# mLSTM gate sums taken once per block for each kind, and rows of z by transposes, in a one-core hybrid decoder trunk

## The chip, the cores and the metric

The kernel runs on one core of a Trainium2 chip. The metric is the device time of one execution in microseconds (us). The engines are named as in the profile: PE is TensorE (matrix products; PEld its weight loads), DVE is VectorE, ACT is ScalarE, POOL is GpSimd, SP is SyncE, whose queue issues most DMAs.

## The reference

One layer of a decoder trunk: an input norm, one input projection of a 1024-token sequence (width 1024, 16 learned meta tokens ahead of it), four mixers side by side (causal pooling, RWKV-7, RG-LRU, mLSTM; 4 heads of 64 each), one output projection, and a squared-ReLU MLP of width 4096, with two norms, all in float32. The part at issue is the mLSTM's gates:

```python
logi = jnp.where(valid, gates[..., :N_H], NEG)
logf = jnp.where(valid, jax.nn.log_sigmoid(gates[..., N_H:]), 0.0)
b = jnp.cumsum(logf, axis=2)                 # prefix sums over the tokens of a chunk
dmat = jnp.where(causal, b[:, :, :, None, :] - b[:, :, None, :, :] + logi[:, :, None, :, :], NEG)
m_intra = jnp.max(dmat, axis=3)              # needs the running maximum of z = logi - b
b_last = b[:, :, -1]                         # the sum over the whole chunk
```

## The kernel before

The 1024 tokens are worked on in 4 blocks of two chunks of 128 tokens; block 0 has the 16 meta tokens as a third, short chunk ahead. A string of steps (PLAN) sets the order in which the program emits its work. The steps of a block are the projection sweeps (S), the pooling (O), the RG-LRU (L), RWKV's preparation (P), its triangular inverse (I), its chunks (C) and outputs (c), mLSTM's gates (M b.0), chunks (M b.1 and on) and outputs (m), and the output projection (W). The first half of the MLP (G, 16 steps) and the first pieces of its second half (D) are put between the steps of the later blocks. After these steps, from about 800 us on, the second half of the MLP runs alone: products of whole tiles at L1189. The build interleaves the emitted steps on each engine; it takes the program as a whole, so an instruction more or less in one step can change how later steps stand against each other.

Large products are made of three: each float32 operand is split into a high and a low part of a reduced format (ACT casts to whi, L127 and L132; DVE subtracts to get wlo, L128 and L133), and high x high, low x high and high x low are summed in PSUM. L476 to L478 are the sweeps' products, L1167 to L1169 the output projection's, L1189 the MLP's. A float32 product outside of that scheme shows as two passes in the trace, a transpose as one; L188 is the transpose of the residual stream.

The change lies in mlstm_pre, the step M b.0. It computes for each chunk the log forget gate lf and the log input gate li, 4 columns (heads) a chunk, tokens on partitions. L952 multiplies by the lower-triangular matrix tri: prefix sums of lf. L953 multiplies by ones: the chunk's total on all partitions. Both write one PSUM tile pb, [128, 2, chunks, 4]; DVE copies it out (L955, L956) and subtracts (z = li - b, L958). L961 turns z into rows, a product with the identity that lands as [4, tokens], and DVE's scan at L964 takes the running maximum from those rows. L967 sums lf into columns. The PSUM tiles of these steps have the tag "l", which has one buffer, so that each of these tiles waits for the reading of the one before. For b = 0 the list `parts` holds the meta rows (16 partitions, chunk 0) and the rest (128 partitions, chunks 1 and 2); for other blocks one part with two chunks.

Two other places come up. The inverse (I) solves a triangular system on DVE (L781 and L782, alternating), stores the result to DRAM (L730, dr<-ys), reads it back in another layout (L733, SA<-dr, and L736, both on SP's queue), transposes it (DVE L739, ys<-SA) and hands it to PE (L748). L1033, L1046 and L1051 are products of mLSTM's chunk, L1040 and L1053 their readers on DVE, L908 to L914 the head norm of its output, whose L140 on POOL is the power -1/2. L1069 transposes that output for the output projection; L1172 adds the projection's result to the residual x. L1220 (POOL's queue) are loads of 1 MB that add a block of weights into DRAM sums (rd<-in_w); L1208 and L1209 add and store other sums (m, md).

Of the kernel before, what the change touches and what calls it, by code (L numbers as in the profile page):

```python
# [16 lines left out]
P = 128  # L17
# [80 lines left out]
class Trunk:  # L98
# [818 lines left out]
    def mlstm_pre(self, b):  # L917

        nc, ml, mp = self.nc, self.mls[b], self.mlp_
        mo, nb, ch = self.block(b)  # L920
        nch = len(ch)
        m = 1 if mo else 0
        li = ml["li"] = mp.tile([P, NTB + 1, NH], F32, name="ml_li", bufs=2)
        lf = ml["lf"] = mp.tile([P, NTB + 1, NH], F32, name="ml_lf", bufs=2)
        bt = ml["b"] = mp.tile([P, NTB + 1, NH], F32, name="ml_b", bufs=2)
        bl = ml["bl"] = mp.tile([P, NTB + 1, NH], F32, name="ml_bl", bufs=2)
        z = ml["z"] = mp.tile([P, NTB + 1, NH], F32, name="ml_z", bufs=2)
        cmr = ml["cm"] = mp.tile([16, NBM], F32, name="ml_g", bufs=2)[0:NH]
        blr = ml["blr"] = mp.tile([NH, NTB + 1], F32, name="ml_blr", bufs=2)
        xf = mp.tile([P, NTB + 1, NH], F32, name="ml_xf")  # L930
        ab = mp.tile([P, NTB + 1, NH], F32, name="ml_ab")
        pg = self.ps("l", [P, nch, 8])
        for ci, (c0, L, _, t) in enumerate(ch):
            nc.tensor.matmul(pg[0:L, ci], lhsT=ml["g"][:, c0:c0 + L], rhs=self.sel, start=True, stop=True)

        if mo:
            nc.vector.memset(li[:, 0], 0.0)
            nc.vector.memset(xf[:, 0], 0.0)
        parts = ([(slice(0, NM), 0, 1)] if mo else []) + [(slice(0, P), m, nch)]
        for rs, i0, i1 in parts:  # L940
            sh = [rs.stop, i1 - i0, NH]
            ifb = self.ifb[rs].rearrange("p (a b) -> p a b", a=1)
            nc.vector.tensor_tensor(li[rs, i0:i1], pg[rs, i0:i1, 0:4], ifb[:, :, 0:4].broadcast_to(sh), op=ALU.add)
            nc.vector.tensor_tensor(xf[rs, i0:i1], pg[rs, i0:i1, 4:8], ifb[:, :, 4:8].broadcast_to(sh), op=ALU.add)
        X = xf[:, 0:nch].rearrange("p a b -> p (a b)")
        AB = ab[:, 0:nch].rearrange("p a b -> p (a b)")
        nc.vector.scalar_tensor_tensor(AB, X, -1.0, X, op0=ALU.mult, op1=ALU.max)
        l1 = self.log1p_exp_neg(AB, [P, nch * NH], mp)
        nc.vector.scalar_tensor_tensor(lf[:, 0:nch].rearrange("p a b -> p (a b)"), X, 0.0, l1, op0=ALU.min, op1=ALU.subtract)
        pb = self.ps("l", [P, 2, nch, NH])  # L950
        for ci, (c0, L, _, t) in enumerate(ch):
            nc.tensor.matmul(pb[0:L, 0, ci], lhsT=self.tri[0:L, 0:L], rhs=lf[0:L, ci], start=True, stop=True)  # L952
            nc.tensor.matmul(pb[:, 1, ci], lhsT=self.ones[0:L].broadcast_to([L, P]), rhs=lf[0:L, ci], start=True, stop=True)  # L953
        for rs, i0, i1 in parts:
            nc.vector.tensor_copy(bt[rs, i0:i1], pb[rs, 0, i0:i1])  # L955
        nc.vector.tensor_copy(bl[:, 0:nch], pb[:, 1])  # L956
        for rs, i0, i1 in parts:
            nc.vector.tensor_tensor(z[rs, i0:i1], li[rs, i0:i1], bt[rs, i0:i1], op=ALU.subtract)  # L958
        pr = self.ps("l", [NH, nb])
        for ci, (c0, L, _, t) in enumerate(ch):  # L960
            nc.tensor.matmul(pr[:, c0:c0 + L], lhsT=z[0:L, ci], rhs=self.ident[0:L, 0:L], start=True, stop=True)  # L961
        for ci, (c0, L, _, t) in enumerate(ch):

            nc.vector.tensor_tensor_scan(cmr[:, c0:c0 + L], pr[:, c0:c0 + L], self.ones[0:NH].broadcast_to([NH, L]), -3.0e38, op0=ALU.max, op1=ALU.mult)  # L964
        pc = self.ps("l", [NH, nch])
        for ci, (c0, L, _, t) in enumerate(ch):
            nc.tensor.matmul(pc[:, ci:ci + 1], lhsT=lf[0:L, ci], rhs=self.ones[0:L], start=True, stop=True)  # L967
        nc.vector.tensor_copy(blr[:, 0:nch], pc)
# [464 lines left out]
```

## Time and profile before

| | |
|---|---|
| median of three runs | 1287.35 us (1285.29, 1292.7, 1287.35) |
| the profiled execution | 1286.41 us, span 1284.6 us |
| mean granted TensorE clock | 0.975 |
| busy: PE, DVE, ACT, POOL | 1223.4, 844.3, 596.0, 108.2 us |
| M b.0's sums (L952, first pass) of blocks 0, 1, 2, 3 at | 222, 302, 507, 639 us |
| PE idle in gaps of at least 0.6 us, 200 to 757 us | 20.6 us in 16 gaps |

A timeline row has start and duration in us, the engine, the line, the operation, the tiles out<-in by the program's names, partitions and shapes, and a count x; in brackets stands the idle time of the engine before it and what ended it. A windows row has the window, its length, each engine's busy time with a count, and then the granted clock of TensorE (1 is full), the share of the DMA engines and their GB/s. Line numbers of the profile are those of the kernel before; behind L951 the changed kernel's are higher by two.

### The profile page before, as it was taken

How to read it: one execution, taken by the hardware profiler on the slowest of the kernel's cores; microseconds unless marked ns; L12 is line 12 of the kernel's file. 1: busy time of each engine (PE TensorE's matmuls, PEld its weight loads, DVE VectorE, ACT ScalarE, POOL GpSimd, SP SyncE). 2: the span in 40 equal slices, each digit the busy share in tenths (PEclk: the TensorE clock that was granted, in tenths of full speed). 3: DMA queues.
4: the chain of work that ended last, by engine and by line, in shares of the span. 5: the costliest groups of instructions: out<-in, count | busy, mean ns of one | idle time of the engine just before them, and what ended most of it. 6: DMA issues, size and time to landing. Idle time of an engine off the chain costs nothing. (4 is left out here: it accounts for less than half of the span.)

```text
span 1284.6 us, 20514 instructions
## 1 busy us (share of the span) xinstructions
PE 1223.4 (95%) x7667; PEld 1048.8 (82%) x7667; DVE 844.3 (66%) x1834; ACT 596.0 (46%) x989; POOL 108.2 (8%) x124
## 2 busy tenths in 40 slices
PE   4999999899988998999999999999999999999997
PEld 3989879789888896777678887888888888888886
DVE  8956475875654766826676689776675566544687
ACT  5432646454346534335334346665565543343330
POOL 4110010200110000001001150000000000000022
PEclk9999888998999998979999999999999999999999
DMA  7546231982898383472655767756657688666662
GB/s 249 186 137 202 77 122 59 218 214 79 205 235 258 124 293 105 147 165 91 164 184 162 261 226 255 253 206 244 239 211 247 214 307 286 196 193 190 190 226 99
DMA packets 123171, 247.90 MB, mean 193 GB/s; under 512 B 28832, under 2 KB 35632, under 8 KB 122944
## 3 DMA queue, kind: packets, MB, share of 16 engines
q1 hardware_dynamic: 114624, 229.82, 53.4%
q0 software_dynamic: 8448, 16.78, 7.7%
q8 instruction: 60, 0.98, 0.3%
q14 instruction: 39, 0.32, 0.1%
HBM read 195.17 MB, written 84.94 MB: 218 GB/s over the span
## 5 line engine op out<-in xcount | busy, mean ns | idle before, releaser
L476 PE MATMUL b<-hTh,whi 128*128 128x256 f32 (+1 forms) x672 | 197.4, 294 | 3.1 <-ACT whi L127 2.0
L133 DVE TENSOR_TENSOR wlo<-wraw,whi 128x1024 fp32r<-128x1024 f32 x112 | 134.1, 1230 | 99.0 <-ACT whi L132 96.8
L478 PE MATMUL b<-hTh,wlo 128*128 128x256 f32 (+1 forms) x672 | 196.3, 293 | 2.8 <-DVE wlo L128 2.7
L477 PE MATMUL b<-hTl,whi 128*128 128x256 f32 (+1 forms) x672 | 197.3, 294 | 0.9 <-DVE hTl L133 0.7
L132 ACT CAST whi<-wraw 128x1024 fp32r<-128x1024 f32 x112 | 113.2, 1051 | 161.1 <-PE bank L1189 139.4
L1189 PE MATMUL bank<-wlo,whi 128*128 128x512 f32 x448 | 175.1, 391 | 1.4 <-DVE wlo L133 1.4
L1189 PE MATMUL bank<-whi,wlo 128*128 128x512 f32 x448 | 174.5, 390 | 0.0
L1189 PE MATMUL bank<-whi 128*128 128x512 f32 x448 | 173.8, 391 | 0.0
L128 DVE TENSOR_TENSOR wlo<-wraw,whi 128x1024 fp32r<-128x1024 f32 x90 | 110.7, 1230 | 76.8 <-ACT whi L127 76.6
L127 ACT CAST whi<-wraw 128x1024 fp32r<-128x1024 f32 x90 | 94.4, 1049 | 128.2 <-PE b L477 50.7
L476 PEld LDWEIGHTS b<-hTh,whi 128*128 128x128 f32 x672 | 130.6, 194 | 6.5 <-ACT whi L127 2.6
L478 PEld LDWEIGHTS b<-hTh,wlo 128*128 128x128 f32 x672 | 130.7, 195 | 5.3 <-DVE wlo L128 3.7
L477 PEld LDWEIGHTS b<-hTl,whi 128*128 128x128 f32 x672 | 130.3, 194 | 2.8 <-DVE hTl L133 1.5
L1189 PEld LDWEIGHTS bank<-wlo,whi 128*128 128x128 f32 x448 | 84.2, 188 | 19.1 <-DVE wlo L133 2.3
L1189 PEld LDWEIGHTS bank<-whi,wlo 128*128 128x128 f32 x448 | 84.1, 188 | 17.4
L1189 PEld LDWEIGHTS bank<-whi 128*128 128x128 f32 x448 | 84.1, 188 | 17.3
L140 POOL TENSOR_TENSOR ln_rs<-ln_rs,mhalf 128x1 f32<-128x1 f32 (+1 forms) x22 | 31.7, 1442 | 601.5 <-DVE ln_rs L139 601.4
L1168 PE MATMUL b<-wlo,mixh 128*128 128x256 f32 x256 | 75.1, 294 | 4.3 <-DVE wlo L128 4.3
L1167 PE MATMUL b<-whi,mixh 128*128 128x256 f32 x256 | 74.5, 293 | 0.5 <-ACT whi L127 0.4
L1169 PE MATMUL b<-whi,mixl 128*128 128x256 f32 x256 | 74.3, 292 | 0.0
L1168 PEld LDWEIGHTS b<-wlo,mixh 128*128 128x128 f32 x256 | 49.8, 195 | 6.7 <-DVE wlo L128 5.7
L1189 PE MATMUL b<-h1Th,whi 128*128 128x512 f32 x128 | 53.4, 424 | 0.7 <-ACT p L1204 0.4
(435 smaller groups left out, 2514.0 us busy)
## 6 DMA issues: line engine op xcount, KB each, us to landing
wraw<-in_w SPq DMA_DIRECT2D x48, 512.0 KB, 4.3
wraw<-in_w_in SPq DMA_DIRECT2D x42, 512.0 KB, 4.7
rd<-in_w POOLq DMA_DIRECT2D x16, 1024.0 KB, 13.3
wraw<-in_w_out SPq DMA_DIRECT2D x32, 512.0 KB, 3.8
wraw<-rd SPq DMA_DIRECT2D x64, 256.0 KB, 4.3
md<-m SPq DMA_DIRECT2D x48, 256.0 KB, 2.3
wraw<-md SPq DMA_DIRECT2D x48, 256.0 KB, 3.1
wraw<-in_w SPq DMA_DIRECT2D x48, 256.0 KB, 4.1
```

Source lines behind the costliest of these rows:

```text
L127: nc.scalar.copy(hi, raw)
L128: (nc.gpsimd if pool else nc.vector).tensor_tensor(lo, raw, hi.bitcast(F32), op=ALU.subtract)
L132: self.nc.scalar.copy(hi, src)
L133: self.nc.vector.tensor_tensor(lo, src, hi.bitcast(F32), op=ALU.subtract)
L140: self.last_pool = nc.gpsimd.tensor_tensor(out, out, self.mhalf[0:rows, 0:w], op=ALU.pow).ins
L476: nc.tensor.matmul(pt, lhsT=wh[:, ks], rhs=hh[:, kt, 0:nb], start=(kt == 0), stop=False)
L477: nc.tensor.matmul(pt, lhsT=wh[:, ks], rhs=hl[:, kt, 0:nb], start=False, stop=False)
L478: nc.tensor.matmul(pt, lhsT=wl[:, ks], rhs=hh[:, kt, 0:nb], start=False, stop=(kt == 7))
L1167: nc.tensor.matmul(pt, lhsT=xh, rhs=wh, start=(kt == 0), stop=False)
L1168: nc.tensor.matmul(pt, lhsT=xh, rhs=wl, start=False, stop=False)
L1169: nc.tensor.matmul(pt, lhsT=xl, rhs=wh, start=False, stop=(kt == 7))
L1189: mm = lambda *p, **k: self.nc.tensor.matmul(*p, skip_group_check=True, **k)
```

## The change

In mlstm_pre the loop over chunks around the two sums becomes a loop over `parts`: the 128-row chunks of a block are handled by one product of each kind, with 8 columns where there were 4, and the meta rows of block 0 by one of each kind as before. Products of the sums: block 0 had 6 and now has 4, the other blocks had 4 and now have 2. The product of z with the identity becomes a call of the transpose. The PLAN and everything else in the source stay as they were.

```diff
-        for ci, (c0, L, _, t) in enumerate(ch):
-            nc.tensor.matmul(pb[0:L, 0, ci], lhsT=self.tri[0:L, 0:L], rhs=lf[0:L, ci], start=True, stop=True)
-            nc.tensor.matmul(pb[:, 1, ci], lhsT=self.ones[0:L].broadcast_to([L, P]), rhs=lf[0:L, ci], start=True, stop=True)
+        for rs, i0, i1 in parts:
+            n, x = rs.stop, lf[rs, i0:i1].rearrange("p a b -> p (a b)")
+            nc.tensor.matmul(pb[rs, 0, i0:i1].rearrange("p a b -> p (a b)"), lhsT=self.tri[rs, 0:n], rhs=x, start=True, stop=True)
+            nc.tensor.matmul(pb[:, 1, i0:i1].rearrange("p a b -> p (a b)"), lhsT=self.ones[rs].broadcast_to([n, P]), rhs=x,
+                             start=True, stop=True)
...
-            nc.tensor.matmul(pr[:, c0:c0 + L], lhsT=z[0:L, ci], rhs=self.ident[0:L, 0:L], start=True, stop=True)
+            nc.tensor.transpose(pr[:, c0:c0 + L], z[0:L, ci], self.ident[0:L, 0:L])
```

Three places show how the built order moves. The first is PE at block 2's gates; L1189 (L1191 in the changed kernel) are the MLP's products around them. Before:

```order
2754 L1189 MATMUL b<-h1Th,wlo 128x512
2755 L952 MATMUL l<-ml_lf,cst 128x4
2756 L953 MATMUL l<-ml_lf,cst 128x4
2757 L952 MATMUL l<-ml_lf,cst 128x4
2758 L953 MATMUL l<-ml_lf,cst 128x4
2759 L1189 MATMUL b<-h1Th,whi 128x512
2760 L1189 MATMUL b<-h1Tl,whi 128x512
2761 L1189 MATMUL b<-h1Th,wlo 128x512
2762 L961 MATMUL l<-cst,ml_z 4x128 x2
2763 L1189 MATMUL b<-h1Th,whi 128x512
```

And after:

```order
2751 L1191 MATMUL b<-h1Th,wlo 128x512
2752 L953 MATMUL l<-ml_lf,cst 128x8
2753 L954 MATMUL l<-ml_lf,cst 128x8
2754 L1191 MATMUL b<-h1Th,whi 128x512
2755 L1191 MATMUL b<-h1Tl,whi 128x512
2756 L1191 MATMUL b<-h1Th,wlo 128x512
2757 L963 MATMUL l<-cst,ml_z 4x128 x2
2758 L1191 MATMUL b<-h1Th,whi 128x512
```

Two of four products are gone; their neighbours are the same.

The second is DVE at the end of block 2's substitution (L781 and L782 alternate; the last L782 is followed by the store of its result). Before:

```order
926 L128 TENSOR_TENSOR wlo<-wraw,whi 128x1024
927 L782 TENSOR_TENSOR ys<-ys,rw_yn 128x8x2
928 L1053 SCALAR_TENSOR_TENSOR ml_num<-l,ml_ae,ml_num 128x65
929 L781 TENSOR_TENSOR rw_yn<-ys,c_5911 128x8
930 L1053 SCALAR_TENSOR_TENSOR ml_num<-l,ml_ae,ml_num 128x65
931 L782 TENSOR_TENSOR ys<-ys,rw_yn 128x8
932 L1053 SCALAR_TENSOR_TENSOR ml_num<-l,ml_ae,ml_num 128x65 x2
933 L1055 SCALAR_TENSOR_TENSOR ml_dn<-ml_num 128x4
```

And after (L1055 and L1057 are the former L1053 and L1055):

```order
926 L1210 TENSOR_TENSOR m_6560<-m_6560 128x512
927 L782 TENSOR_TENSOR ys<-ys,rw_yn 128x8x2
928 L781 TENSOR_TENSOR rw_yn<-ys,c_5905 128x8
929 L782 TENSOR_TENSOR ys<-ys,rw_yn 128x8
930 L1055 SCALAR_TENSOR_TENSOR ml_num<-l,ml_ae,ml_num 128x65 x4
931 L1057 SCALAR_TENSOR_TENSOR ml_dn<-ml_num 128x4
```

The last L782 stood behind two of the four readers of mLSTM's product and now stands ahead of all four. The wlo (L128) that stood five rows ahead of it comes later, among L908 and L909, ahead of the row that feeds POOL's L140.

The third is block 3's inverse. PE around L748, before:

```order
3298 L1051 MATMUL l<-C_305,ml_q 128x130 x2
3299 L1167 MATMUL b<-whi,mixh 128x256
3300 L1168 MATMUL b<-wlo,mixh 128x256
3301 L1169 MATMUL b<-whi,mixl 128x256
3302 L1167 MATMUL b<-whi,mixh 128x256
3303 L1168 MATMUL b<-wlo,mixh 128x256
3304 L1169 MATMUL b<-whi,mixl 128x256
3305 L1167 MATMUL b<-whi,mixh 128x256
3306 L1168 MATMUL b<-wlo,mixh 128x256
3307 L1169 MATMUL b<-whi,mixl 128x256
3308 L748 MATMUL r<-ys,p_6758 32x32 x16
```

And after, where L1169 to L1171 are the former L1167 to L1169, and L1048 the former L1046:

```order
3305 L1170 MATMUL b<-wlo,mixh 128x256
3306 L1171 MATMUL b<-whi,mixl 128x256
3307 L1169 MATMUL b<-whi,mixh 128x256
3308 L748 MATMUL r<-ys,p_6752 32x32 x16
3309 L1170 MATMUL b<-wlo,mixh 128x256
3310 L1048 MATMUL l<-ml_vo,ml_e 128x65 x4
3311 L1171 MATMUL b<-whi,mixl 128x256
```

L748 stood behind the chunk's products L1046 and L1051; now both come behind it. On DVE, the reader that L748 waits for (L739), before:

```order
1163 L1012 SCALAR_TENSOR_TENSOR ml_ar<-ml_b,l 128x4
1164 L128 TENSOR_TENSOR wlo<-wraw,whi 128x1024
1165 L1026 TENSOR_TENSOR ml_kw<-l,ml_we 128x256
1166 L1172 SCALAR_TENSOR_TENSOR x<-x,b 128x256 x2
1167 L1053 SCALAR_TENSOR_TENSOR ml_num<-l,ml_ae,ml_num 128x65 x2
1168 L739 STREAM_TRANSPOSE ys<-SA 128x256
```

And after:

```order
1159 L1014 SCALAR_TENSOR_TENSOR ml_ar<-ml_b,l 128x4
1160 L1174 SCALAR_TENSOR_TENSOR x<-x,b 128x256
1161 L128 TENSOR_TENSOR wlo<-wraw,whi 128x1024
1162 L739 STREAM_TRANSPOSE ys<-SA 128x256
1163 L1028 TENSOR_TENSOR ml_kw<-l,ml_we 128x256
```

L739 stood behind two readers of L1051's product and now stands behind the second of the adds x<-x,b and one wlo.

## The prediction

> **What bounds the kernel now.** I read the page first (busy shares), then windows, the waits of the lines that the change touches, and the timelines where those lines stand and where PE waits.
>
> ```profile
> PE 1223.4 (95%) x7667; PEld 1048.8 (82%) x7667; DVE 844.3 (66%) x1834; ACT 596.0 (46%) x989; POOL 108.2 (8%) x124
> 800.00:1100.00 300.00, 300.00 (x1325) 248.31 (x1324) 197.09 (x253) 166.38 (x242) 0.00 (x0) 1.00 0.70 244
> ```
>
> PE is busy for 95% of the span, and from 800 to 1100 us (the last row: length, busy time of PE, weight load, DVE, ACT, POOL, then clock, DMA share, GB/s) it has no gap at all, at clock 1.00. So a microsecond of work taken from PE is a microsecond of the span unless something else holds PE there. What remains is PE idle time and stretches with a lower granted clock, of which rows stand below. Who waits for those lines:
>
> ```profile
>   DVE ml_b L955: 6.5, 4
>   DVE ml_g L964: 2.8, 3
> ```
>
> These are DVE's waits for L953 and for L961, over all blocks. DVE is 66% busy, and PE itself does other work behind L953 and L961, so a shorter answer to DVE there is no gain of its own.
>
> **The sums (L951 to L953).** PE's timeline in block 3 (start, duration, line; x2 is two passes of one fp32 product), and one group over all blocks:
>
> ```profile
> 638.98 0.35 PE L952 MATMUL l<-ml_lf,cst 128*128 128x4 f32 x2
> 639.20 0.36 PE L953 MATMUL l<-ml_lf,cst 128*128 128x4 f32 x2
> 639.42 0.36 PE L952 MATMUL l<-ml_lf,cst 128*128 128x4 f32 x2
> 639.64 0.36 PE L953 MATMUL l<-ml_lf,cst 128*128 128x4 f32 x2
> 639.87 0.48 PE L1189 MATMUL b<-h1Tl,whi 128*128 128x512 f32 x1
> L952 PE MATMUL l<-ml_lf,cst x18: 162/252/273, 221.9 to 639.5; 128*128 128x4 f32 x16, 16*16 16x4 f32 x2
> ```
>
> Starts are (639.87 - 638.98)/4 = 0.22 us apart: that is what one such product takes of PE's time, its longer duration being overlap. The 18 passes are 9 products a kind, 18 in all. The change leaves 4 in block 0 (the meta rows stay apart) and 2 in each of blocks 1 to 3, 10 in all. The 8 that go save 8 x 0.22 = 1.8 us. The two that stay in a block have 8 columns, not 4. No row has 128x8; the nearest are these with 4, and L1021's with 128 columns:
>
> ```profile
> 653.81 0.27 PE L1021 MATMUL l<-cst,ml_v 128*128 128x128 f32 x1
> 653.92 0.27 PE L1022 MATMUL l<-cst,ml_k 128*128 128x128 f32 x1
> ```
>
> One pass with 128 columns follows the other by 0.11 us, half of 0.22 for two passes with 4: the columns do not show in the spacing. So I take nothing for four more columns; the upper end, were they to cost in proportion, is another 0.22 for each of the 8 wide products, 1.8 us, which would eat this saving.
>
> **The rows of z (L961).** In block 3 and in block 0:
>
> ```profile
> 641.18 0.60 PE L961 MATMUL l<-cst,ml_z 128*4 128x128 f32 x4
> 223.29 0.85 PE L188 MATMUL b<-cst,x 128*128 128x128 f32 x6
> 224.07 0.73 PE L961 MATMUL l<-cst,ml_z 16*4 16x16 f32 x6
> 224.73 0.44 PE L188 MATMUL b<-cst,x 128*128 128x128 f32 x2
> ```
>
> A product is two passes here as well: 4 for two chunks, 6 for three. L188 is this kernel's transpose, one pass each; six take 224.07 - 223.29 = 0.78 us, 0.13 each. L961's six passes take 224.73 - 224.07 = 0.66, 0.11 each. Nine products lose one pass each: 9 x 0.13 = 1.2 us by L188's spacing, 9 x 0.11 = 1.0 by its own; I take 1.15. The lower end is none, if the transpose costs two passes' time (a rival, below).
>
> The direct sum is 1.8 + 1.15 = 2.95 us of PE, 0.23% of the time. DVE, ACT and POOL issue as many instructions as before, and SP as many DMAs.
>
> **Does the clock hold through the transposes?** The window with block 0's transposes (L188, above):
>
> ```profile
> 220.00:230.00 10.00, 9.51 (x85) 8.02 (x84) 5.47 (x20) 4.94 (x13) 0.00 (x0) 1.00 0.56 169
> ```
>
> The granted clock stays 1.00 around the transposes at 223 to 225 us. So I charge two transposes in the midst of full products nothing. [...]
>
> **What the shift moves.** PE's order changes beyond the edited lines: from block 2's gates (507 us) to about 757 us the steps interleave differently; before and behind, the neighbours are the same. Three places count.
>
> Block 2's inverse. PE, DVE, SP and POOL, the median landing of such a load, and the windows:
>
> ```profile
> 555.12 1.06 PE L748 MATMUL r<-ys,p 32*32 32x32 f32 x32 [2.52 <-DVE ys L739]
> 554.62 0.45 DVE L739 STREAM_TRANSPOSE ys<-SA 128x256 f32<-128x256 f32 x1 [4.28 <-DMA SA<-dr]
> 539.60 0.17 DVE L782 TENSOR_TENSOR ys<-ys,rw_yn 128x8 f32<-128x8 f32 x1
> 544.45 0.33 SPq L1209 DMA_DIRECT2D md<-m  x1
> 544.96 2.04 SPq L733 DMA_DIRECT2D SA<-dr  x4
> 544.34 0.17 DVE L139 TENSOR_SCALAR ml_rs<-ml_sm 128x4 f32<-128x4 f32 x1
> 545.54 2.12 POOL L1220 DMA_DIRECT2D rd<-in_w  x2
> SA<-dr SPq DMA_DIRECT2D x16, 32.0 KB, 2.3
> 549.66 0.69 DVE L1208 TENSOR_TENSOR m<-m 128x512 f32<-128x512 f32 x1
> 550.00:560.00 10.00, 7.48 (x96) 5.29 (x96) 2.29 (x4) 3.47 (x8) 0.00 (x0) 0.75 1.21 203
> 560.00:570.00 10.00, 10.00 (x50) 7.70 (x49) 0.82 (x4) 4.00 (x10) 0.00 (x0) 0.50 0.66 224
> ```
>
> PE waits 2.52 us for DVE's L739, and that for the DMA SA<-dr, whose last part lands 7.6 us after its last issue (544.96 + 2.04 = 547.00; to 554.62), where the median is 2.3. Two adding loads of 1 MB go out from POOL at 545.54, in the midst of its four pieces. After the wait the clock is 0.50 from 560 to 570 us. What that costs:
>
> ```profile
> 561.10 0.63 PE L1189 MATMUL b<-h1Th,wlo 128*128 128x512 f32 x1
> 561.53 0.63 PE L1189 MATMUL b<-h1Th,whi 128*128 128x512 f32 x1
> 638.37 0.39 PE L1189 MATMUL b<-h1Th,wlo 128*128 128x512 f32 x1
> 638.60 0.39 PE L1189 MATMUL b<-h1Th,whi 128*128 128x512 f32 x1
> ```
>
> The same product stands every 0.43 us there and every 0.23 at full clock, so of some 16 us at half clock (555.5 to about 572) 16 x (1 - 0.23/0.43) = 7.4 are lost. Counted from the end of the substitution (539.77), SA<-dr was issued by 7.2 us and the first adding load went out at 5.8. In the new order DVE's row that feeds POOL's L140, and through it those loads, comes later: all four L1053, one wlo and the add L1208 now stand between. One wlo is 1.2 us, L1208 0.7; the PE product that L1053 reads (L1051) comes five L1189 later, 5 x 0.23 = 1.1. So the loads come 2 to 3 us later, at 7.8 to 8.8 (an estimate). SA<-dr comes no later, and perhaps some tenths earlier, since md<-m, which went out at 544.45 just ahead of it, is now behind it on SP's queue. Then its four pieces are issued before the loads rather than among them and land by 539.8 + 7.2 + 2.3 = 549.3. L739 then goes when DVE comes to it, behind L1208: 550.4 by the row above. PE was there at 555.12 - 2.52 = 552.6 and comes some 1.1 earlier (48 products of L1189 behind L1051 for 58, 5 more ahead of it), at 551.5. DVE's later head norm may push L739 from 550.4 to 551 or 552, so a wait of 0 to 1 us is left of 2.52. Shorter waits were not followed by half clock:
>
> ```profile
> 276.64 0.41 PE L1069 MATMUL l<-cst,ml_yn 128*128 128x128 f32 x2 [1.18 <-DVE ml_yn L914]
> 276.00:286.00 10.00, 9.36 (x132) 8.88 (x135) 6.84 (x17) 4.04 (x9) 0.03 (x1) 1.00 0.66 183
> ```
>
> The bounds are -9.9 (wait and half clock gone) and +1.1 (the loads still meet SA<-dr and PE waits from an earlier time). I take -2.0 for the wait, 0.5 being left, and -6 for the clock: of 7.4 some comes back where PE, now faster, meets the next wlo. The sign rests on the order of two queues; the size on the clock, which no order shows.
>
> Block 3's inverse. No wait before:
>
> ```profile
> 675.17 0.69 PE L748 MATMUL r<-ys,p 32*32 32x32 f32 x32
> 666.76 1.84 SPq L733 DMA_DIRECT2D SA<-dr  x4
> 655.50 0.45 PE L1033 MATMUL l<-ml_vo,ml_kw 128*64 128x65 f32 x8
> 674.73 0.28 PE L1167 MATMUL b<-whi,mixh 128*128 128x256 f32 x1
> 674.84 0.28 PE L1168 MATMUL b<-wlo,mixh 128*128 128x256 f32 x1
> ```
>
> PE came 19.2 us after L1033 ended (675.17 - 655.95). In the new order I count between them 67 of W_out's products, 0.12 apart by the rows of L1167 and L1168 (8.0 us), 12 of L1189 at 0.23 (2.8) and some 4.8 us of mLSTM's own: 15.6 us, an estimate, so PE would be at L748 at an equivalent 671.5. SA<-dr needs 666.76 + 1.84 + 2.3 = 670.9, and L739 takes 0.43 more: 671.3, 0.2 us to spare. Nothing as it stands; but if SA<-dr were as late as in block 2 (7.6 for 2.3 us), the wait would be up to 5. I take 0.3, with ends 0 and 3, and half clock behind it as a rival.
>
> Block 3's output product and exchange (700 to 757 us) changes its neighbours too; no single wait there decides, and I take zero, within 2 either way (the size of block 2's whole wait).
>
> **The wait at 370 us.**
>
> ```profile
> 370.50 0.50 PE L1069 MATMUL l<-cst,ml_yn 128*128 128x128 f32 x2 [4.12 <-DVE ml_yn L914]
> ```
>
> The saving of blocks 0 and 1, 0.45 + 0.33 + 0.45 + 0.26 = 1.5 us (four products of 0.22, and 3 + 2 passes), reaches the end only if what ends this wait also moves up; it follows DVE work that PE feeds, so I let it. If not, 1.5 of 2.95 is left.
>
> **The sum.** The profiled execution took 1286.41 us, 0.94 below the median 1287.35 of the runs shown. 1286.41 - 2.95 + 0.3 = 1283.8 with block 2's stall as it was; less 2.0 and 6 it is 1275.8, and I put 1276.0. A change of 0.5%, 6.4 us, is about what a measurement of this kernel can tell from no change (the three runs lie 7.4 apart): 1280.9 to 1293.8 around the median.
>
> **Rivals.** *Block 2's stall stays.* Then only the products go: 1283.8, 1281 to 1287 with the small terms. For it: the loads have to come 1.5 us later at least, and my 2 to 3 is counted from one execution's times. *A wait in block 3 with half clock behind it.* For it: PE comes 3.7 us sooner with 0.2 to spare, and 2.52 us was enough in block 2. Against: its SA<-dr took no harm before, and only SP's order, not POOL's, changes around it. It decides from about 2 us of lateness of SA<-dr: 2 to 3 us of wait and 5 to 8 of clock (10 to 16 us at half clock). With block 2's stall also there it gives 1283.8 + 7 to 11 = 1291 to 1295, slower; with that gone, 1283 to 1287, no change. [...] *A transpose takes two passes' time, or blocks 0 and 1 lose their share to the wait at 370:* 1 to 1.5 us less gain, on top of whichever case holds.
>
> **How the numbers follow.** Block 2's stall goes and nothing comes: 0.42, its own range 1273 to 1280, all faster. It stays and nothing comes: 0.34. It goes and block 3's comes: 0.10, both of these same. It stays and block 3's comes: 0.11, of which 0.08 above 1293.8. Transposes and clock: 0.03. Faster 0.42; same 0.34 + 0.10 + 0.03 = 0.47; slower 0.08 + 0.03 = 0.11. Same is the likelier verdict, but it is made of several cases; the likeliest single one is the forecast. The range 1273 to 1290 leaves out the slower two, 0.14, and some 0.03 below.
>
> **What the profile after would show.** L953 and L954 with 10 passes each for 18, 0.22 us apart; L963 with 9 for 18, 0.11 to 0.13 apart; PE busy less by about 3 us; clock 1.00 around 224 and 641. Block 2's SA<-dr issued before POOL's two rd<-in_w and landing within about 3 us, its L748 with a wait of under 1 us, and clock near 1.00 in the 15 us behind; block 3's L748 with under 0.5. I am wrong if block 2's L748 still waits over 2 us, if half clock stands behind it in any case, if block 3's waits over 2, or if a new gap of over 2 us stands between 700 and 757.

## The result, and the profile after

The changed kernel took 1273.75 us (median of 18 runs, 1266.25 to 1287.99), the kernel before 1283.06 beside it (18 runs, 1278.21 to 1292.7). The ratio is 0.9923, with a 95% interval of 0.9901 to 0.9946: 9.9 us less, between 6.9 and 12.7. It goes by the fast runs alone, without the one of 1287.99 us, so it is not the ratio of these two medians. The profiled execution took 1273.62 us, at a mean clock of 0.983 where the one of before had 0.975.

The head of its page:

```profile
span 1271.8 us, 20464 instructions
PE 1208.1 (95%) x7642; PEld 1036.5 (81%) x7642; DVE 844.4 (66%) x1834; ACT 594.5 (47%) x989; POOL 110.1 (9%) x124
```

PE is busy for 15 us less, five times the work that was taken out; its share stays 95%. L1189's products followed each other by 0.23 us at full clock and by 0.43 at half clock in the profile of before (at 638.37 and at 561.10 us), so most of that is clock, not work.

The products themselves, PE's timeline in block 0 and block 2 and the groups of the two lines (L953 was L952, L963 was L961):

```profile
216.11 0.39 PE L953 MATMUL l<-ml_lf,cst 128*128 128x8 f32 x2
216.36 0.37 PE L954 MATMUL l<-ml_lf,cst 128*128 128x8 f32 x2
216.58 0.85 PE L188 MATMUL b<-cst,x 128*128 128x128 f32 x6
217.36 0.49 PE L963 MATMUL l<-cst,ml_z 16*4 16x16 f32 x3
217.69 0.82 PE L188 MATMUL b<-cst,x 128*128 128x128 f32 x6
...
500.31 0.28 PE L953 MATMUL l<-ml_lf,cst 128*128 128x8 f32 x2
500.45 0.37 PE L954 MATMUL l<-ml_lf,cst 128*128 128x8 f32 x2
500.68 0.48 PE L1191 MATMUL b<-h1Th,whi 128*128 128x512 f32 x1
L953 PE MATMUL l<-ml_lf,cst x10: 162/252/278, 215.7 to 626.2; 128*128 128x8 f32 x8, 16*16 16x4 f32 x2
L963 PE MATMUL l<-cst,ml_z x9: 174/272/273, 217.4 to 627.9; 128*4 128x128 f32 x8, 16*4 16x16 f32 x1
```

Ten passes of L953 stand where 18 stood, nine of L963 where 18 stood. With 8 columns a sum takes 0.25 and 0.22 us in block 0, and the pair 0.37 in block 2, where the four products of 4 columns took 0.80 (507.32 to 508.12). Three transposes take 217.69 - 217.36 = 0.33, 0.11 each.

Block 2's inverse, on DVE, SP, POOL and PE, and the two windows that were at 0.75 and 0.50:

```profile
531.42 0.17 DVE L782 TENSOR_TENSOR ys<-ys,rw_yn 128x8 f32<-128x8 f32 x1
536.99 1.81 SPq L733 DMA_DIRECT2D SA<-dr  x4
539.59 2.12 POOL L1222 DMA_DIRECT2D rd<-in_w  x2
542.64 0.44 DVE L739 STREAM_TRANSPOSE ys<-SA 128x256 f32<-128x256 f32 x1
543.99 0.69 PE L748 MATMUL r<-ys,p 32*32 32x32 f32 x32
550.00:560.00 10.00, 9.99 (x97) 8.36 (x96) 3.44 (x8) 3.97 (x9) 0.00 (x0) 1.00 1.08 300
560.00:570.00 10.00, 9.78 (x84) 8.32 (x82) 4.74 (x14) 4.51 (x12) 1.03 (x1) 1.00 0.10 32
```

SA<-dr is through its issue at 538.80, 0.8 us ahead of the first adding load, where before the load went out in its midst. L739 and L748 wait for nothing, and the clock stays at 1.00.

And a wait of PE that was not there before, at 700 us. PE, DVE, and SP's queue, and last the same DVE row in the kernel before:

```profile
702.67 0.47 PE L1191 MATMUL bank<-whi 128*128 128x512 f32 x1 [2.56 <-DVE ys L896]
700.33 0.61 DVE L895 SCALAR_TENSOR_TENSOR ys<-r,prm,rw_bv 128x128 f32<-128x128 f32 x2 [4.84 <-DMA yd<-ys]
693.72 0.38 SPq L591 DMA_DIRECT2D yd<-ys  x1
695.51 7.04 SPq L124 DMA_DIRECT2D wraw<-in_w_out  x2
...
711.60 0.61 DVE L895 SCALAR_TENSOR_TENSOR ys<-r,prm,rw_bv 128x128 f32<-128x128 f32 x2 [2.40 <-DMA yd<-ys]
```

DVE's L895 writes RWKV's second output tile into the one buffer "ys" and waits for the store of the first, issued at 693.72. In the kernel before, DVE waited for the same store too, 2.40 us, but PE had other work to do meanwhile; now DVE waits 4.84 and PE with it.

To set the two kernels side by side, the program is cut at block 2's gates (first L952, now L953), at L748 of blocks 2 and 3, and at W_out's last product with mixh, which stands here:

```profile
745.24 0.28 PE L1169 MATMUL b<-whi,mixh 128*128 128x256 f32 x1
```

In the kernel before it is at 758.77. Four profiled executions of each kernel (before, base2, base3, base4; after, again2, again3, again4, below) give these lengths in us:

| stretch | before | changed | difference of means |
|---|---|---|---|
| start to block 0's gates (nothing changed) | 221.9, 222.7, 220.4, 219.8 | 215.7, 218.2, 221.6, 215.5 | -3.5 |
| to block 2's gates | 285.4, 283.2, 288.0, 281.9 | 284.6, 284.7, 284.0, 285.3 | 0.0 |
| to L748 of block 2 | 47.8, 49.0, 48.1, 48.8 | 43.7, 43.7, 43.8, 43.7 | -4.7 |
| to L748 of block 3 | 120.0, 120.0, 119.0, 116.1 | 114.2, 114.2, 116.9, 114.5 | -3.8 |
| to the last product of W_out | 83.6, 82.5, 84.6, 83.6 | 87.0, 87.1, 85.1, 85.4 | +2.6 |
| to the start of PE's last product | 517.7, 518.2, 518.3, 517.9 | 518.4, 517.8, 518.0, 517.6 | -0.1 |

L748 itself changed its place among PE's products: in block 2 four products of L1189 (0.9 us) that stood ahead of it now stand behind it. So of the -4.7 some 3.1 are the wait, 0.7 the products taken out, and 0.9 only moved to the next stretch. Between block 2's gates and W_out's end the change is worth 5.9 us (250.8 to 244.8 in the mean); each kernel's four lie within 3.2 and 2.2 us. The -3.5 ahead of it lies where both kernels issue the same instructions in the same order.

That whole stretch as one window, before and after:

```profile
507.32:758.77 251.45, 243.67 (x1661) 198.22 (x1660) 160.50 (x446) 100.19 (x185) 28.72 (x31) 0.97 0.59 174
500.31:745.24 244.93, 235.93 (x1649) 191.84 (x1648) 161.27 (x446) 99.90 (x185) 30.67 (x31) 0.99 0.60 177
```

PE's idle time, the length less its busy time, is 7.8 us before and 9.0 after (8.4 and 8.7 in the mean of the four). So the wait at block 2's L748 went, but other waits took its place, and PE idles no less. What fell is the work, by 1.4 us, and the time at half clock: 17, 17, 14 and 7 us in the four executions of the kernel before, 3, 3, 7 and 0 in those of the changed one. By L1189's 0.23 and 0.43 us, 1 - 0.23/0.43 = 0.465 of the time at half clock is lost, which makes about 4.8 us in the mean (an estimate).

### The profile page after: what moved, and what is told of

It reads as the page before. It is cut to its first block, busy times and chain, and to the rows that moved or that the text cites. A ratio compares the mean times of both kernels' runs of the same rounds, so it can differ in the third digit from the quotient of the medians.

```text
span 1271.8 us, 20464 instructions
## 1 busy us (share of the span) xinstructions
PE 1208.1 (95%) x7642; PEld 1036.5 (81%) x7642; DVE 844.4 (66%) x1834; ACT 594.5 (47%) x989; POOL 110.1 (9%) x124
## 4 chain that ended last, share of the span: by engine, by line
PE 75%; DVE 8%; DMA 7%; issue 4%; ACT 4%; POOL 2%; SPq 1%; DVEq 0%; ACTq 0%; POOLq 0%
PE bank L1191 39%; PE b L1191 6%; PE b L477 5%; PE b L478 4%; PE b L476 4%; DMA wraw<-in_w_out 2%; DVE wlo L128 2%; PE r L694 2%; PE b L1170 1%; PE b L1169 1%; PE b L1171 1%; DMA wraw<-in_w 1%; ACT whi L127 1%; DMA yd<-ml_num 1%; POOL rw_rn L140 1%
## 5 line engine op out<-in xcount | busy, mean ns | idle before, releaser
L1191 PE MATMUL bank<-whi 128*128 128x512 f32 x448 | 175.0, 392 | 2.6 <-DVE ys L896 2.6
L1191 PE MATMUL bank<-wlo,whi 128*128 128x512 f32 x448 | 175.6, 392 | 1.3 <-DVE wlo L133 1.3
L1191 PE MATMUL bank<-whi,wlo 128*128 128x512 f32 x448 | 175.3, 391 | 0.0
L128 DVE TENSOR_TENSOR wlo<-wraw,whi 128x1024 fp32r<-128x1024 f32 x90 | 111.0, 1235 | 76.1 <-ACT whi L127 75.6
L1191 PEld LDWEIGHTS bank<-whi 128*128 128x128 f32 x448 | 84.6, 189 | 20.0 <-issue 3.0
L1191 PEld LDWEIGHTS bank<-wlo,whi 128*128 128x128 f32 x448 | 84.5, 189 | 19.1 <-DVE wlo L133 1.9
L1191 PEld LDWEIGHTS bank<-whi,wlo 128*128 128x128 f32 x448 | 84.5, 189 | 17.4
L140 POOL TENSOR_TENSOR ln_rs<-ln_rs,mhalf 128x1 f32<-128x1 f32 (+1 forms) x22 | 32.8, 1495 | 611.1 <-DVE ln_rs L139 611.0
L1169 PE MATMUL b<-whi,mixh 128*128 128x256 f32 x256 | 73.3, 289 | 0.9 <-ACT mixh L132 0.9
L1171 PE MATMUL b<-whi,mixl 128*128 128x256 f32 x256 | 72.6, 287 | 0.0
L1170 PEld LDWEIGHTS b<-wlo,mixh 128*128 128x128 f32 x256 | 48.8, 191 | 6.5 <-DVE wlo L128 5.3
L1191 PE MATMUL b<-h1Th,wlo 128*128 128x512 f32 x128 | 52.3, 411 | 0.5 <-DVE wlo L128 0.5
## 6 DMA issues: line engine op xcount, KB each, us to landing
rd<-in_w POOLq DMA_DIRECT2D x16, 1024.0 KB, 13.5
```

The source lines that it names most:

```text
L128: (nc.gpsimd if pool else nc.vector).tensor_tensor(lo, raw, hi.bitcast(F32), op=ALU.subtract)
L140: self.last_pool = nc.gpsimd.tensor_tensor(out, out, self.mhalf[0:rows, 0:w], op=ALU.pow).ins
L1169: nc.tensor.matmul(pt, lhsT=xh, rhs=wh, start=(kt == 0), stop=False)
L1170: nc.tensor.matmul(pt, lhsT=xh, rhs=wl, start=False, stop=False)
L1171: nc.tensor.matmul(pt, lhsT=xl, rhs=wh, start=False, stop=(kt == 7))
L1191: mm = lambda *p, **k: self.nc.tensor.matmul(*p, skip_group_check=True, **k)
```

## The experiments

Theory A: most of the gain is the wait at block 2's L748 and the half clock behind it; they went because the two loads of 1 MB now go out behind SA<-dr. Theory B: the gain is the PE work alone, the rest chance. Each ratio below is to runs of the kernel before that were timed beside it; their median was 1287.58 us for sums, transp, late and way, 1281.26 for y1 and 1284.98 for z0.

**sums.** The sums of the change alone; L961 stays a product. The order at block 2's inverse is that of before.

```diff
+        for rs, i0, i1 in parts:
+            n, x = rs.stop, lf[rs, i0:i1].rearrange("p a b -> p (a b)")
...
             nc.tensor.matmul(pr[:, c0:c0 + L], lhsT=z[0:L, ci], rhs=self.ident[0:L, 0:L], start=True, stop=True)
```

> Only the sums are changed (one product of each kind for all 128-row chunks), the rows of z stay products. Two theories. Theory A: most of the gain is block 2's wait at L748 with the half clock behind it, which went because the two 1 MB loads now go out behind SA<-dr. Theory B: the gain is PE work alone (products and transposes), the rest is chance. The built order at block 2's inverse is that of the kernel before here. A: L748 of block 2 waits 2 to 3 us as before, DMA SA<-dr lands 5 us or more late, and the time is 1283 - 1.8 = about 1281 (ratio 0.998 to 1.000). B: 8 of the 12.5 products' worth of work go, so about six tenths of the 9.3 us: 1277 to 1278 (ratio 0.995 to 0.996), whatever L748 does.

Measured: 1282.55 us, ratio 0.9951 (0.9921 to 0.9982). PE, SP, POOL and the window behind:

```profile
557.51 0.69 PE L748 MATMUL r<-ys,p 32*32 32x32 f32 x32 [2.94 <-DVE ys L739]
546.97 2.01 SPq L733 DMA_DIRECT2D SA<-dr  x4
547.55 2.12 POOL L1222 DMA_DIRECT2D rd<-in_w  x2
560.00:570.00 10.00, 10.00 (x93) 8.04 (x93) 2.32 (x5) 4.29 (x10) 0.00 (x0) 0.50 0.79 239
```

The load goes out in the midst of SA<-dr, PE waits 2.94 us and half clock follows: with the old order comes the old stall, whatever PE was spared. The time alone does not decide; its interval holds B's value and just touches A's. It fell by more than the 1.8 us that A allows, by 5.0 between the means. By the mean clock of each run the kernel was at half clock for 59.9 us, the runs of before for 66.0: at 0.465 lost of each us that is 2.8 (an estimate), and it is not shown whether this difference of clock is chance.

**transp.** The transposes alone; the sums stay as before. The order at block 2's inverse is that of the changed kernel.

```diff
-            nc.tensor.matmul(pr[:, c0:c0 + L], lhsT=z[0:L, ci], rhs=self.ident[0:L, 0:L], start=True, stop=True)
+            nc.tensor.transpose(pr[:, c0:c0 + L], z[0:L, ci], self.ident[0:L, 0:L])
```

> Only the rows of z are changed (transposes), the sums stay as before. The built order at block 2's inverse is that of the changed kernel. A: L748 of block 2 waits under 1 us, SA<-dr is issued before the two loads of 1 MB; of the 9.3 us only the sums' 1.8 are missing, so 1274 to 1277 (ratio 0.993 to 0.995). B: only nine passes of 0.11 to 0.13 us go, 1.15 us: 1282 (ratio 0.998 to 1.000).

Measured: 1278.6 us, ratio 0.9931 (0.9907 to 0.9954). SP, POOL, PE and the window:

```profile
539.22 1.81 SPq L733 DMA_DIRECT2D SA<-dr  x4
541.82 2.12 POOL L1220 DMA_DIRECT2D rd<-in_w  x2
546.22 0.69 PE L748 MATMUL r<-ys,p 32*32 32x32 f32 x32
560.00:570.00 10.00, 10.00 (x93) 8.64 (x91) 3.93 (x12) 3.40 (x9) 1.02 (x1) 1.00 0.32 120
```

Some 1 us less of PE work brings nearly the whole gain, with no wait and no half clock. B's 0.998 lies outside the interval.

**late.** The kernel before, with the two loads moved behind block 3's preparation. PE, DVE and SP keep the order of before.

```diff
+for z in ("A", 4, 1), ("A", 4, 0):
+    STEPS.remove(z)
+    STEPS.insert(STEPS.index("P3") + 1, z)
```

> The kernel before, with all its products, and with one thing moved: the two loads of 1 MB of block 2's inverse go out on POOL's queue behind the next square root but two, some 60 us later. The order of PE, DVE and SP is that of the kernel before. A: SA<-dr lands within about 3 us, L739 goes when DVE comes to it (10.6 us behind the last L782), PE's wait at L748 of block 2 is under 0.5, no half clock behind it; 1283 - 2.5 - 3 to 6 = 1275 to 1278 (ratio 0.994 to 0.996). B: no PE work is saved, so 1283 (ratio 0.999 to 1.001).

Measured: 1282.41 us, ratio 0.9955 (0.9926 to 0.9985). SP, POOL, PE at block 2's L748 (L751 here; SA<-dr is L736), its window, and a later place on PE and ACT:

```profile
547.36 2.03 SPq L736 DMA_DIRECT2D SA<-dr  x4
602.67 3.15 POOL L1223 DMA_DIRECT2D rd<-in_w  x3
554.90 0.69 PE L751 MATMUL r<-ys,p 32*32 32x32 f32 x32
560.00:570.00 10.00, 10.00 (x95) 8.44 (x92) 2.60 (x7) 4.05 (x9) 0.00 (x0) 1.00 0.37 120
629.28 0.61 PE L937 MATMUL l<-cst,ml_g 16*128 16x8 f32 x4 [2.67 <-ACT ml_num L1074]
626.99 1.04 ACT L130 CAST whi<-wraw 128x1024 fp32r<-128x1024 f32 x1 [4.56 <-DMA wraw<-in_w]
```

With every product of before, block 2's wait and half clock are gone, and the time falls as A expects. Three loads now go out together near 603 us, and PE waits 2.67 us at 629 for ACT, which waited for a weight load: part of the gain is given back there. That the three loads made the weight load late is likely, not shown.

**way.** The changed kernel, with the two loads put ahead of SA<-dr again. PE, DVE and SP keep the order of the changed kernel.

```diff
-        nc.gpsimd.memset(X64[0:32, :, 32:64], 0.0)
+        self.inv_pool = nc.gpsimd.memset(X64[0:32, :, 32:64], 0.0).ins
...
-            with self.tc.issue_after(self.last_pool):
+            with self.tc.issue_after(self.inv_pool if i == 4 and j < 2 else self.last_pool):
```

> The changed kernel, with one thing moved: the two loads of 1 MB go out right behind POOL's memset at the end of block 2's substitution, ahead of SA<-dr, not behind the head norm's square root. The order of PE, DVE and SP is that of the changed kernel. A: SA<-dr lands late again (5 us or more), PE waits 2 us or more at L748 of block 2 and the clock falls behind it; the time is 1273.75 + 2.5 to 8 = 1276 to 1282 (ratio to before 0.995 to 0.999). B: the PE work is still saved, so 1273 to 1275 (ratio 0.992 to 0.994).

Measured: 1287.07 us, ratio 1.0022 (0.9996 to 1.0049): the whole gain is gone. POOL, SP, DVE, PE and the window:

```profile
537.99 2.12 POOL L1222 DMA_DIRECT2D rd<-in_w  x2
550.05 1.82 SPq L733 DMA_DIRECT2D SA<-dr  x4
555.39 0.45 DVE L739 STREAM_TRANSPOSE ys<-SA 128x256 f32<-128x256 f32 x1 [6.90 <-DMA XT<-dr]
555.89 1.07 PE L748 MATMUL r<-ys,p 32*32 32x32 f32 x32 [6.06 <-DVE ys L739]
550.00:560.00 10.00, 4.11 (x84) 3.20 (x85) 0.45 (x1) 1.93 (x6) 0.00 (x0) 0.75 0.99 262
```

The loads went out further ahead than in the kernel before, beside the store dr<-ys, and SA<-dr, which reads what that store writes, was issued only at 550.05, 12 us after them. What ended the wait was XT<-dr (L736), the second half of the reading back, issued right behind SA<-dr. PE waits 6.06 us, and the time lies above A's range. B expected no loss at all. late and way together show what causes the stall: the same two transfers, moved alone, take the stall away from the old kernel and bring a longer one to the new.

**y1.** An attempt at a faster version: the changed kernel with the second chunk's output tile in another buffer.

```diff
-        y1 = rcp.tile([P, 2, P], F32, name="ys")
+        y1 = rcp.tile([P, 2, P], F32, name="SA" if ci % 2 else "ys")
```

> The changed kernel, with the output tile y1 of RWKV's second chunk in the buffer of SA, not in that of ys, so that the second y1 no longer waits for the store of the first, nor POOL's memset of block 2's Y for the store of the second. Theory A (waits of PE set the time where they are long): the wait of 3.7 us at L1071 near 359 us and the one of 2.56 at 702.67 shrink to under 1 each, with the half clock behind them: 3 to 8 us less, 1266 to 1271 against 1273.75 (ratio to before 0.986 to 0.991). Against it: the built order moves again from 310 us on, and block 3's L748 comes 18 rows earlier on PE, so that a new wait there can eat the gain. Theory B: such waits only move: ratio 0.991 to 0.995, as the changed kernel.

Measured: 1274.34 us, ratio 0.9926 (0.989 to 0.9961), no different from the changed kernel. The wait at 702 us is gone, but the order moved, and from L748 of block 3 to W_out's end it takes 89.6 us, more than any above. At 359 us, on POOL, DVE and PE, then the changed kernel's PE row:

```profile
346.98 2.17 POOL L140 TENSOR_TENSOR ln_rs<-ln_rs,mhalf 128x1 f32<-128x1 f32 x2 [5.22 <-DVE ln_rs L139]
353.74 0.42 DVE L912 TENSOR_REDUCE ml_sm<-ml_kw 128x4 f32<-128x256 f32 x1 [2.28 <-ACT ml_kw L911]
358.07 0.61 PE L1071 MATMUL l<-cst,ml_yn 128*128 128x128 f32 x2 [3.74 <-DVE ml_yn L914]
```

```profile
358.81 0.54 PE L1071 MATMUL l<-cst,ml_yn 128*128 128x128 f32 x2 [3.70 <-DVE ml_yn L914]
```

POOL no longer waits for the store, and PE waits as long as ever: what is late now is DVE's head norm itself, which waits for ACT behind L910. Theory A's second half falls here; a wait that has another one right behind it only changes its name.

**again2, base2, base3, again3, base4, again4.** Both kernels unchanged, further profiled executions.

> The changed kernel once more, for a second look at what in one profile belongs to the kernel and what to the one execution. A: block 2's L748 waits under 0.5 us again, the wait of 2.5 us at 702 us is there again, the half clock near 223, 236, 360, 400 and 490 us may lie elsewhere.

> The kernel before once more. A: block 2's L748 waits 2 to 3 us again with half clock behind it, SA<-dr lands 5 us or more late; the time before the first changed line (222 us) differs by some us from the first profile, since nothing there is tied to the change.

> The kernel before, a third look. The stretch from block 2's gates to the last product of W_out took 251.4 and 251.5 us in two looks, and 244.9 and 245.0 in two of the changed kernel. If that difference is the mechanism (block 2's wait and its half clock, less the new wait at 702 us), this look gives 251 to 252. The first 222 us, where nothing differs, took 221.9 and 222.7 here, 215.7 and 218.2 in the changed kernel: if that is the window of the clock falling here or there by chance, looks of both kernels mix between 215 and 224; if the kernels differ there by something not seen, this one is again at 222 or above.

> The changed kernel, a third look. Mechanism: 244.5 to 245.5 us from block 2's gates to the last product of W_out. Chance in the first 222 us: anywhere from 215 to 224; something not seen: 215 to 218.

> The kernel before, a fourth look, as the third: 251 to 252 us from block 2's gates to the last product of W_out by the mechanism; the first 222 us anywhere from 215 to 224 by chance, 222 or above if the kernels differ there.

> The changed kernel, a fourth look, as the third: 244.5 to 245.5 us by the mechanism; the first 222 us anywhere from 215 to 224 by chance, 215 to 218 if the kernels differ there.

Measured: 1275.64, 1285.48, 1288.33, 1279.36, 1278.06 and 1272.02 us; the stretches stand in the table. Block 2's wait was there in every execution of the kernel before (2.52, 3.68, 2.90, 3.48 us) and in none of the changed kernel. From block 2's gates to W_out's end the kernel before took 251.4, 251.5, 251.7 and 248.5, the changed one 244.9, 245.0, 245.8 and 243.6, outside of the expected 244.5 to 245.5 in two. The one that misses 251 is base4, where the wait is long and the half clock behind it short:

```profile
550.49 0.70 PE L748 MATMUL r<-ys,p 32*32 32x32 f32 x28 [3.48 <-DVE ys L739]
555.00:560.00 5.00, 5.00 (x32) 3.57 (x33) 0.50 (x3) 2.10 (x6) 0.00 (x0) 0.73 0.76 288
```

The first 222 us go by the clock and not by the kernel. PE's idle time there is 23.5 to 25.4 us in all fourteen traces (those of the other experiments included), while the time at half clock runs from 3.4 to 23.9 us. In the traces of before and after, every change of the granted clock lies a whole number of steps of 3.41 us from the others (half clock begins at 145.42, 172.72, 193.21, 240.99 us and on in before, at 34.69, 222.42, 236.07 and on in after), and the clock behind block 0's sums in the other twelve fits a grid of the same step. Where that grid lies against the first instruction differs from execution to execution. Four executions of four kernels in which it lies at 1.98 to 2.11 us (again3, z0, before, way) took 221.6 to 221.9; the four at 0.16 to 0.91 or at 3.15 (again4, after, transp, y1) took 214.9 to 216.5; the six between took 218.2 to 224.3. So the 3.5 us between the means go with where the grid lies, as far as fourteen executions show.

**z0.** The changed kernel with block 0's rows of z by products.

```diff
+            if mo:
+                nc.tensor.matmul(pr[:, c0:c0 + L], lhsT=z[0:L, ci], rhs=self.ident[0:L, 0:L], start=True, stop=True)
+            else:
                 nc.tensor.transpose(pr[:, c0:c0 + L], z[0:L, ci], self.ident[0:L, 0:L])
```

> The changed kernel, with the rows of z of block 0 alone by products as before (three products, six passes), those of blocks 1 to 3 by transposes; the order at block 2's inverse stays that of the changed kernel. Asked: does it come from block 0's transposes that all seven looks with them show about 3.5 us of half clock 6 to 10 us behind block 0's sums, where two of six looks without them do? If the transposes bring it on, this look has full clock from 6 to 10 us behind the sums. If it is chance, or the removed sums' doing, the half clock is there. In either case block 2's L748 has no wait, and the time is that of the changed kernel within 2 us, since 0.33 us of PE come back and at most 1.7 go (ratio to before 0.990 to 0.995).

Measured: 1274.79 us, ratio 0.9919 (0.9887 to 0.9952), as the changed kernel. The windows behind block 0's sums, of the changed kernel (sums at 215.7), of way (at 221.9) and of z0 (at 221.8):

```profile
220.00:225.00 5.00, 4.61 (x28) 3.99 (x29) 3.80 (x13) 1.66 (x7) 0.00 (x0) 0.74 0.96 293
225.00:230.00 5.00, 5.00 (x39) 4.24 (x38) 3.23 (x10) 0.78 (x3) 2.05 (x3) 0.92 0.41 118
...
225.00:230.00 5.00, 4.54 (x36) 3.79 (x33) 3.70 (x14) 2.35 (x9) 0.00 (x0) 0.74 0.86 256
```

```profile
225.00:230.00 5.00, 4.51 (x42) 3.83 (x42) 3.94 (x14) 3.06 (x11) 0.00 (x0) 1.00 0.89 250
230.00:235.00 5.00, 4.79 (x41) 3.99 (x39) 4.44 (x13) 1.03 (x4) 2.30 (x3) 1.00 0.63 197
```

Half clock begins 5 to 8 us behind block 0's sums in seven of seven executions with transposes there and in two of seven without. Where block 0's sums fall at the same place on that grid (1.2 to 1.4 us into it), the executions divide cleanly: way and again3, with transposes, have it; before, sums and z0, with products, don't. From block 0's gates to block 1's these two took 82.8 us each, the other three 80.2, 79.4 and 79.4, though transposes are less work (0.11 us each, where a product's two passes took 0.22). That speaks strongly for the transposes bringing it on; z0 is still one execution, and in the times of whole runs (0.9919 against 0.9923) it does not show.

## Why the prediction was right, step by step

**The direct sum.** Its sizes hold: 0.22 a sum with 8 columns as with 4, 0.11 a transpose, 10 and 9 passes. The upper bound for the wider columns was not needed. Whether all 2.95 us arrive is another matter: from block 0's gates to block 2's, where 1.5 of them lie, the means are equal. The prediction let that share pass the wait at 370 us; these stretches do not show that it did, since the kernel before varies there by 6 us, and the changed kernel was at half clock there for 31.6 us in the mean, the other for 27.3. An estimate over whole runs speaks for it. A run of T us at mean clock c is at half clock for 2 x (1 - c) x T, since the traces of before and after show 1.00 and 0.50 and nothing between, and loses 0.465 of that. The 17 runs of the changed kernel that the ratio goes by, 1274.4 us in the mean, come to 1253.3 without that loss; the runs of the kernel before beside the experiments come to 1256.2, 1256.4 and 1256.9. That is 2.9 to 3.6 us of gain without the clock, about the direct sum; the rest of the gain is time at half clock.

**Block 2's wait.** This step carried the forecast, and it was right in its mechanism and in its times. Loads 7.8 to 8.8 us behind the end of the substitution: 539.59 - 531.59 = 8.0. SA<-dr issued by 7.2: 538.80 - 531.59 = 7.2. L739 at 10.6 to 12.2: 542.64 - 531.59 = 11.1. A wait of 0.5 was to be left; none was. late and way show that the loads are the cause. But the -2.0 for the wait is no net gain: from block 2's gates to W_out's end PE idles as long as before.

**The clock behind it.** Taken as -6 of 7.4; the stretch that holds it is shorter by 3.8 in the mean, 5.8 between the first two profiles. Time at half clock fell there from 13.5 to 1.7 us in the mean, worth 5.5 (an estimate), and 1.4 us of new idle time took some of it back. The half clock behind block 2's wait is not of one length (base4), and the forecast took one execution's for the kernel's.

**Block 3's wait.** Put at 0.3, rival at 0.21: L748 of block 3 waits 0.1 us at most in every execution of either kernel.

**700 to 757 us.** "I take zero, within 2 either way" was the step that failed: +2.6 in the mean. PE's idle time from block 3's L748 to W_out's end is 1.9 to 3.5 us in the four executions of the kernel before and 4.3 to 5.3 in those of the changed one. Its main chain was readable: the store yd<-ys and the one buffer "ys" stood in the code, and DVE's wait of 2.40 us for it in the trace of before. The prediction named a gap of over 2 us there as a sign of being wrong, and in two of four executions it came (2.56 and 2.02); in the other two the idle time is spread over waits of up to 1.6.

**Transposes and clock.** The clock was expected at 1.00 around 224 us and fell to 0.74 (220 to 225 us). The prediction gives 0.03 to a loss of clock by the transposes. No run shows one at all four places: in the changed kernel the clock is 1.00 from 294 to 314, from 500 to 520 and from 626 to 646 us, behind the sums of blocks 1 to 3, and the profiled execution took 1273.62 us where 1276.0 was forecast. But the row of before by which the transposes were charged nothing did not bear it: that one execution had full clock there, and base2, the same kernel, had half clock from 230.0 to 233.4 us, 7.3 behind its block 0's sums. What speaks for block 0's transposes bringing it on is the seven of seven, and the clean division at one place of the grid; neither proves it.

**The sum.** The steps as measured give -5.9 us from block 2 on, where they were forecast at about -9. That the total nonetheless came out at -9.9, where -10.4 was forecast (1286.41 to 1276.0), is luck in part. Between -5.9 and the -9.9 of the many runs lie 4 us, 1 to 7 by the interval, that four traces of each kernel do not place; by the estimate above they are the missing share of the direct sum and time at half clock somewhere else, on which no step of the prediction rests.

## What to carry to other kernels

Where a build fits the whole program together, a small saving early can be worth less than the order that it shifts: read which transfers stand around each long wait, on all queues, and ask on which side of them they come out in the new order. Then prove it by moving those transfers alone, once out of the old kernel's way and once into the new one's. Reckon the clock behind a wait apart from its length: here PE idled as long after the change as before, and the gain was the half clock and the products. And follow every place whose order moves as far as the one you like: the wait that came at 700 us was as readable as the one that went at 555.

## What the runs showed of the hardware that was not expected

**One profile is one draw of the clock.** The same instructions took 215 to 224 us to block 0's gates, by half-clock stretches near 30, 145, 175 and 195 us that come in some executions and not in others, according to where the grid of 3.41 us falls. Of the changed kernel's runs one took 1266.25 us at a mean clock of 0.989, another 1282.53 at 0.975: 16.3 us for 0.014, about 1.2 us for each 0.001 between these two. In the traces of before and after, up to the last 5 us, half clock stood in stretches of 3.41, 6.83, 10.24 and 17.07 us, that is 1, 2, 3 and 5 steps of that grid.

**Small transfers behind large ones.** In the kernel before, the four pieces of 32 KB of block 2's SA<-dr, whose median is 2.3 us, took 7.6 with two loads of 1 MB let in among them, and in way, with the loads beside the store ahead of them, they were issued only 12 us after the loads.
